# Sixteen gate weight tiles multiplied as eight pairs by seven block products

## The chip, the cores and the metric

The kernel runs on one core of a Trainium2 chip. Its time is the device time of one execution in microseconds (us); a kernel's time is the median of its runs. The engines named below are TensorE (PE, with its weight load PEld), VectorE (DVE), ScalarE (ACT), GpSimd (POOL) and SyncE (SP, which here only issues DMAs). Each engine works through its own instructions in order and waits for the others through semaphores.

## The reference, cut to what matters

One layer of a hybrid block: two token mixers over 512 latent tokens (after 256 context tokens), a gated merge of both, a residual with modulation, and a feed-forward stage. Width is 1024, all in fp32. The change touches the products of `u` (the normalised and modulated input) with the gate weights and what hangs on them:

```python
def merge(pp, o, h):                      # pp: the columns of u @ w_in
    y_gla = _head_rms_norm(o, gla_norm_g, u.dtype) * jax.nn.silu(pp[3])
    y_m = h * jax.nn.sigmoid(pp[8])
    gate_gla, gate_m = jnp.split(jax.nn.sigmoid(pp[10]), 2, axis=-1)
    y = gate_gla * (y_gla @ w_br_gla) + gate_m * (y_m @ w_br_mlstm)
    return y @ w_out
x = x + g1 * mix
x = x + g2 * _swiglu(_modulate(_rms_norm(x, norm2_g[i]), sh2, sc2), w_ffn_in[i], w_ffn_out[i])
```

`h` is the mLSTM scan's result; this scan runs over the tokens in column-major order. The vectors `g1`, `sh2`, `sc2`, `g2` are rows of `silu(c) @ w_ada + b_ada` (adaLN).

## The kernel before

**Products.** Features lie on the 128 partitions and tokens along the free axis. A fp32 factor is split into a high part (fp32r) and a low remainder, and a product is three matmuls, hi·hi, hi·lo and lo·hi (`mm3`, L243 to L245). A weight tile of 1024x128 is loaded by SP into a raw buffer (`wload`, L220, three buffers), ACT casts it to `whi` (L215), DVE subtracts to get `wlo` (L216); there are four buffers of each. A gate (`gate`, L880) is one weight tile against all 512 tokens: 8 times 3 matmuls of 512 columns into `ps_g`, then a sigmoid on ACT (L885 to L887). `u` stands in `ub`, from L929 on as `ucm`: 8 tiles in column-major token order, in each 512 columns of high and 512 of low part.

**Order of the stages.** At the start (to about 56 us) an order written by hand, the table `ORDER`, runs the modulation rows (`M..`, and the transposes `R0` to `R3` of their results into columns, L359), the normalisation and the steps that make `u` (`ut`, `uh`, `ul` and so on). Then come the projections and both scans. `head_norm` normalises the scan's output `mo`: an inverse root by Newton steps on 128x8 values (L178 to L180) and eight scalings (L666), each of 128x256. `to_feat` (L893) transposes the scan's output back to features and multiplies it with its gate and norm weight (`yf`, L902), and splits it: `yg` for the first branch, `ym` for the second.

Then `branch_a` (L983) runs eight times: a wp10 gate, a `wbg` product of `yg`, and their product `ya` (L989). `interleave` puts the 32 adaLN rows between its steps, four rows each (`ada_rows`, L968): SP loads 512 KB into `wr`, POOL multiplies with `crow` (L972), ACT sums up along the row into a column of `ada` (L973). Behind it stand eight wp8 gates (`p8`), `to_feat(mo, ...)` for `ym`, and eight times a wp10 gate, a `wbm` product of `ym`, their product and the sum with `ya` (branch B, `yb`). The output product `ps_wo`, the residual and the feed-forward stage follow. That stage multiplies pairs of 128-column weight tiles already by seven block products instead of eight (`Pair`, `prod`, `pair_slot`), with the order of PE, DVE and ACT written by hand (`tc.manual_schedule`).

**Who sets the order.** Outside such stretches a scheduler decides, with a model of the engines' times, where each instruction stands on its engine; it is fixed when the kernel is built. Buffers come from pools by tag: `blk` has 29 buffers for all its uses, `mid` 8, `tmp` 7; PSUM has four banks for `psm` and four for `psx`. A new tile waits until the last reader of the buffer's old tile is done.

Of the kernel before, what the change touches and what calls it, by code (L numbers as in the profile page):

```python
# [69 lines left out]
def block_kernel(ctx: ExitStack, tc: tile.TileContext, a, out):  # L70
# [818 lines left out]
    def halves(n, nm):  # L889
        bl_ = [blk(f"{nm}{i}") for i in range((n + 1) // 2)]  # L890
        return [bl_[i // 2][:, (i % 2) * 512:(i % 2) * 512 + 512] for i in range(n)]

    def to_feat(o_pairs, gate_, v0, nm):  # L893

        ys = []
        for j in range(8):
            ps = psx("ps_t" + nm)
            for t in range(4):
                o = (t % 2) * 512 + (j % 4) * P
                pe.transpose(ps[:, t * P:(t + 1) * P], o_pairs[j // 4][t // 2][:, o:o + P], ident)  # L900
            y = tmp("yf")[:, :512]
            vec.scalar_tensor_tensor(y, ps, vc(v0 + j), gate_[j], op0=ALU.mult, op1=ALU.mult)  # L902
# [95 lines left out]
    p8 = halves(8, "p8_")  # L998
# [124 lines left out]
    def prod(ps, w, x, first):

        for k in range(4):
            c, t = slice(k * P, k * P + P), slice(k * 256, k * 256 + 256)
            for i, (y, z) in enumerate(((0, 0), (0, 1), (1, 0))):
                pe.matmul(ps[:, :256], lhsT=w[y][:, c], rhs=x[z][:, t], start=first and k + i == 0,  # L1134
                          stop=k == 3 and i == 2, skip_group_check=not first)

    def flat(t):
        return t.rearrange("p k c -> p (k c)")

    class Pair:  # L1140


        def __init__(self, j):
            self.j = j
            self.raw = [flat(wload(a["wfi"][2 * j + i])[0]) for i in range(2)]
            self.b11, self.b21 = self.raw[0][:, :512], self.raw[0][:, 512:]
            self.b12, self.b22 = self.raw[1][:, :512], self.raw[1][:, 512:]
            self.g = {}

        def sums(self):  # L1150
            self.t21, self.t34 = blk("t21")[:, :1024], blk("t34")[:, :1024]
            self.t2, self.t1 = self.t21[:, :512], self.t21[:, 512:]
            self.t3, self.t4 = self.t34[:, :512], self.t34[:, 512:]

        def t(self, n):
            o, p_, q_ = {1: (self.t1, self.b11, self.b12), 2: (self.t2, self.t1, self.b22),
                         3: (self.t3, self.b12, self.b22), 4: (self.t4, self.t2, self.b21)}[n]
            vec.tensor_tensor(o, p_, q_, op=ALU.add)  # L1158

        def hi(self, n, early=False):  # L1160

            if n == 4:
                g4 = blk("g4", F32R)
                h, l, src = (g4[:, :512],), (g4[:, 512:1024],), (self.b22,)
            elif early:
                src = {1: lambda: (self.b11, self.b21), 2: lambda: (self.t2, self.t1)}[n]()
                h, l = ([bp.tile([P, EW], F32R, name=f"e{n}", tag="mid", bufs=8)[:, :512] for _ in range(2)]
                        for _ in range(2))
            else:
                src = ({1: lambda: self.raw[0], 2: lambda: self.t21, 3: lambda: self.t34}[n](),)  # L1170
                h = (flat(wp.tile([P, NK, P], F32R, name=f"g{n}h", tag="whi", bufs=NHI)),)
                l = (flat(wp.tile([P, NK, P], F32R, name=f"g{n}l", tag="wlo", bufs=NLO)),)
            self.g[n] = (h, l, src)
            for x, y in zip(h, src):
                act.copy(x, y)

        def lo(self, n):
            for h, l, src in zip(*self.g[n]):
                vec.tensor_tensor(l, src, h.bitcast(F32), op=ALU.subtract)

        def half(self, n, i=0):

            if len(self.g[n][0]) > 1 or n == 4:
                return self.g[n][0][i], self.g[n][1][i]
            return self.g[n][0][0][:, 512 * i:512 * i + 512], self.g[n][1][0][:, 512 * i:512 * i + 512]
# [298 lines left out]
```

## Time and profile before

| | before |
|---|---|
| median of 3 runs | 1093.02 us (1092.85 to 1093.86) |
| the profiled execution | 1093.14 us |
| its span in the trace | 1091.4 us |
| PE busy | 1070.8 us (98%), 5882 matmuls |
| DVE busy | 676.6 us (62%) |
| ACT busy | 536.8 us (49%) |
| POOL busy | 114.0 us (10%), of it the 32 adaLN rows 89.8 us |
| chain that ended last | PE 88%, DVE 4%, DMA 3%, ACT 2% |

The profile is one execution seen instruction by instruction. A row of its timeline reads: start and duration in us, engine, line, operation, output<-inputs by the program's names, shapes, count, and in brackets how long the engine had been idle before it and what ended that. `q` behind an engine's name is its queue of DMA issues. In this notation branch A runs until 549 us, the wp8 gates to 594, branch B from there to 686, the output product and the rest to the end.

### The profile page before, as it was taken

To read this page: it belongs to the slowest core of one execution; us is meant where nothing else is said; L and a number is where in the kernel's file an instruction comes from. 1 tells how busy PE (TensorE), PEld (TensorE's weight loads), DVE (VectorE), ACT (ScalarE), POOL (GpSimd) and SP (SyncE) were. 2 spreads that over 40 slices of the span, in tenths; PEclk is the share of its full clock that TensorE was granted. 3 is DMA by queue.
4 is the path that set the end of the run, shared out by engine and by line. 5 is a ranking of instruction groups with operands and counts; after the bars stand their busy time and mean duration, and the time that the engine had idled before them with its cause. 6 is when DMAs were issued, how large, how long until landed. Compare 5 with 4: busy or idle time off the path is not lost.

```text
span 1091.4 us, 14985 instructions
## 1 busy us (share of the span) xinstructions
PE 1070.8 (98%) x5882; PEld 909.3 (83%) x5882; DVE 676.6 (62%) x1192; ACT 536.8 (49%) x902; POOL 114.0 (10%) x57
## 2 busy tenths in 40 slices
PE   9899999999999999999999999999899999999996
PEld 3578888788888888888888888899899999988886
DVE  4867785964384484694234544569888888873333
ACT  5577655543272365366563323356565555742211
POOL 0000100200010000049980000000000000110000
PEclk9899999999999999999999999999999999999999
DMA  9612111021121121257764223601332333333212
GB/s 362 230 58 69 47 44 43 12 105 39 42 76 38 37 93 65 72 184 287 250 211 134 77 96 97 243 28 36 120 106 90 115 117 110 99 110 103 87 53 77
DMA packets 34270, 116.39 MB, mean 107 GB/s; under 512 B 3960, under 2 KB 6264, under 8 KB 34200
## 3 DMA queue, kind: packets, MB, share of 16 engines
q1 hardware_dynamic: 32672, 114.25, 31.1%
q10 hardware_dynamic: 1528, 1.19, 0.3%
q8 instruction: 46, 0.75, 0.3%
q14 instruction: 24, 0.20, 0.1%
HBM read 113.33 MB, written 2.10 MB: 106 GB/s over the span
## 4 chain that ended last, share of the span: by engine, by line
PE 88%; DVE 4%; DMA 3%; ACT 2%; issue 1%; SPq 0%; DVEq 0%; ACTq 0%
PE ps_X L1134 10%; PE ps_g L245 5%; PE ps_g L244 5%; PE ps_g L243 5%; PE ps_Z L1134 5%; PE ps_fo L245 4%; PE ps_fo L243 4%; PE ps_fo L244 4%; PE ps_v L428 3%; PE ps_v L430 3%; PE ps_v L429 3%; PE ps_br L245 3%; PE ps_br L244 3%; PE ps_br L243 3%; PE ps_Y L1134 2%; PE ps_mU L836 2%
## 5 line engine op out<-in xcount | busy, mean ns | idle before, releaser
L216 DVE TENSOR_TENSOR wlo<-wraw,whi 128x1024 fp32r<-128x1024 f32 (+1 forms) x110 | 140.8, 1283 | 142.6 <-ACT whi L215 141.2
L215 ACT CAST whi<-wraw 128x1024 fp32r<-128x1024 f32 (+1 forms) x110 | 113.2, 1035 | 184.3 <-PE ps_fo L244 71.1
L244 PE MATMUL ps_g<-ucm,whi 128*128 128x512 f32 x256 | 102.6, 401 | 0.0
L245 PE MATMUL ps_g<-ucm,wlo 128*128 128x512 f32 x256 | 102.0, 398 | 0.0
L243 PE MATMUL ps_g<-ucm,whi 128*128 128x512 f32 x256 | 101.5, 397 | 0.0
L972 POOL TENSOR_TENSOR wr<-wr,crow 128x1024 f32<-128x1024 f32 x32 | 89.8, 2842 | 65.8 <-ACT crow L965 65.8
L243 PE MATMUL ps_fo<-h,whi 128*128 128x512 f32 (+1 forms) x198 | 73.4, 371 | 0.0
L244 PE MATMUL ps_fo<-h,whi 128*128 128x512 f32 (+1 forms) x198 | 72.9, 369 | 0.0
L245 PE MATMUL ps_fo<-h,wlo 128*128 128x512 f32 (+1 forms) x198 | 72.9, 369 | 0.0
L244 PEld LDWEIGHTS ps_g<-ucm,whi 128*128 128x128 f32 x256 | 48.1, 188 | 11.2
L243 PEld LDWEIGHTS ps_g<-ucm,whi 128*128 128x128 f32 x256 | 48.1, 188 | 10.9
L245 PEld LDWEIGHTS ps_g<-ucm,wlo 128*128 128x128 f32 x256 | 48.1, 188 | 10.5
L973 ACT ACTIVATE wr<-wr 128x1024 f32<-128x1024 f32 x32 | 33.9, 1060 | 35.6 <-POOL wr L972 35.6
L1330 POOL TENSOR_TENSOR h<-hf,h 128x512 fp32r<-128x512 f32 x5 | 7.8, 1559 | 389.7 <-ACT h L1329 389.7
L244 PEld LDWEIGHTS ps_fo<-h,whi 128*128 128x128 f32 x198 | 37.2, 188 | 6.9
L245 PEld LDWEIGHTS ps_fo<-h,wlo 128*128 128x128 f32 x198 | 37.2, 188 | 6.8
L243 PEld LDWEIGHTS ps_fo<-h,whi 128*128 128x128 f32 x198 | 37.2, 188 | 6.8
L682 POOL TENSOR_SCALAR_AFFINE_SELECT a<-a 128x512 f32<-128x512 f32 x8 | 10.9, 1365 | 202.7 <-ACT a L679 202.6
L1134 PE MATMUL ps_Z<-s5h,g 128*128 128x256 f32 x160 | 31.6, 280 | 0.0
L1246 DVE TENSOR_TENSOR hf<-sl,cc 128x512 f32<-128x512 f32 x20 | 14.9, 747 | 23.4 <-ACT sl L1245 23.3
L1245 ACT ACTIVATE sl<-ps_X 128x256 f32<-128x256 f32 x20 | 7.7, 385 | 41.7 <-PE ps_X L1134 41.7
L1158 DVE TENSOR_TENSOR t<-t,wraw 128x512 f32<-128x512 f32 x40 | 27.6, 689 | 0.7
(475 smaller groups left out, 3157.1 us busy)
## 6 DMA issues: line engine op xcount, KB each, us to landing
wraw<-in_wfi SPq DMA_DIRECT2D x44, 512.0 KB, 3.6
wraw<-in_wp SPq DMA_DIRECT2D x32, 512.0 KB, 3.5
wr<-in_wada_b SPq DMA_DIRECT2D x32, 512.0 KB, 4.7
wa<-in_wada_a SPq DMA_DIRECT2D x16, 512.0 KB, 9.2
wraw<-in_wfo SPq DMA_DIRECT2D x16, 512.0 KB, 3.5
wraw<-in_wgv SPq DMA_DIRECT2D x8, 512.0 KB, 3.6
wraw<-in_wmqk SPq DMA_DIRECT2D x8, 512.0 KB, 3.5
wraw<-in_wmv SPq DMA_DIRECT2D x8, 512.0 KB, 4.1
```

Of the source, the lines that this page charges most:

```text
L215: act.copy(hi, src)
L216: vec.tensor_tensor(lo, src, hi.bitcast(F32), op=ALU.subtract)
L243: pe.matmul(ps, lhsT=wh, rhs=xh, start=first, stop=False)
L244: pe.matmul(ps, lhsT=wh, rhs=xl, start=False, stop=False)
L245: pe.matmul(ps, lhsT=wl, rhs=xh, start=False, stop=last)
L428: pe.matmul(ps, lhsT=h_, rhs=wh, start=(k == 0), stop=False)
L429: pe.matmul(ps, lhsT=h_, rhs=wl, start=False, stop=False)
L430: pe.matmul(ps, lhsT=l_, rhs=wh, start=False, stop=(k == NK - 1))
L972: pool.tensor_tensor(wr, wr, crow, op=ALU.mult)
L973: act.activation(wr, wr, AF.Identity, accum_out=ada[:, j:j + 1])
L1134: pe.matmul(ps[:, :256], lhsT=w[y][:, c], rhs=x[z][:, t], start=first and k + i == 0, stop=k == 3 and i == 2, skip_group_check=not first)
L1158: vec.tensor_tensor(o, p_, q_, op=ALU.add)
```

## The change

Four parts. First, the eight wp8 gates and the second eight wp10 gates are taken as eight pairs, in `gate_slot`, each with seven products of a 512x128 weight block and 256 tokens (12 matmuls of 256 columns each). Such a product needs sums of weight blocks (`Pair`, whose class moves up unchanged but for its source) and four sums and differences of token blocks, `su[1]`, `su[2]`, `su[3]`, `su[5]`. Second, a generator `s_gen` makes the token sums; it is chained behind `ada_rows` as the filler of branch A, and the rate goes from 4 to 6.5. `su[3]` is written over a part of `ucm` that is read no more (`s3_split`). Third, all gates come first: the transposes and products for `ym` are run within slots 5 and 6 and behind slot 7 (`feat_gen`), and then the eight `wbm` products, without gates between them. Fourth, in `ORDER`, `R0` and `T0` move up and three warm-up steps (matmuls on constants, nothing reads their result) are put in.

```diff
-    SQ5 ... M03 R2 ut7 ut6 uh7 T2
-    ut2 R0 uh6 ul7 T0 uh2 ul6 g7 S0 ...
+    SQ5 ... M03 R2 R0 ut7 ut6 uh7 T2
+    warm T0 warm warm ut2 uh6 ul7 uh2 ul6 g7 S0 ...
...
+    def s_gen():
...
+        f, f3 = blk("sf")[:, :1024], blk("sf3")[:, :1024]
+        gs[3] = f3
+        def diff(o, x, y):
+            d = tmp("sd")[:, :512].rearrange("p (h t) -> p h t", h=2)
+            vec.tensor_tensor(d, x, y, op=ALU.subtract)
+            vec.tensor_tensor(o, d[:, 0], d[:, 1], op=ALU.add)
+        def halve(n):
+            su[n] = [(units.pop(0), units.pop(0)) for _ in range(4)]
+            for k in range(4):
+                act.copy(su[n][k][0], f[:, 256 * k:256 * k + 256])
+                vec.tensor_tensor(su[n][k][1], f[...], su[n][k][0].bitcast(F32), op=ALU.subtract)
+        for k in range(4):
+            diff(f[:, 256 * k:256 * k + 256], part(k, B), part(k + 4, B))
+            yield
+        halve(1)
+        yield
+        for k in range(4):
+            diff(f3[:, 256 * k:256 * k + 256], part(k, A), part(k, B))
+            yield
+        for n, o, op in ((2, 0, ALU.subtract), (5, 4, ALU.add)):
+            for k in range(4):
+                for h in range(2):
+                    c = f[:, 256 * k:256 * k + 256]
+                    vec.tensor_tensor(c, c, part(k + o, A)[:, h], op=op)
+                yield
+            halve(n)
+            yield
+    def s3_split():
+        su[3] = [(ub[k][:, 256:512], ub[k][:, 768:1024]) for k in range(4)]
+        for k in range(4):
+            c = gs[3][:, 256 * k:256 * k + 256]
+            act.copy(su[3][k][0], c)
+            vec.tensor_tensor(su[3][k][1], c, su[3][k][0].bitcast(F32), op=ALU.subtract)
+    def gate_slot(w, nx, late, o0, o1):
...
+        prod(X, w.half(1), U11, True)
+        late()
+        act.copy(p1, X[:, :256])
...
+        prod(Y, w.half(1, 1), U12, True)
+        vec.tensor_tensor(p1, Y[:, :256], p1, op=ALU.add)
...
+        prod(X, w.half(2), su[2], False)
+        act.copy(u2, X[:, :256])
+        act.activation(o0[:, A], p1, AF.Sigmoid)
...
+        prod(Z, w.half(2, 1), su[1], True)
+        act.copy(q5, Z[:, :256])
...
+        prod(X, w.half(3), su[3], False)
+        act.copy(u3, X[:, :256])
...
+        vec.tensor_tensor(cc[:, B], q5, u3, op=ALU.subtract)
+        prod(Z, w.half(4), su[5], False)
+        vec.tensor_tensor(cc[:, A], Z[:, :256], u2, op=ALU.subtract)
+        prod(X, w.half(3, 1), U22, False)
+        def end():
+            act.activation(o0[:, B], X[:, :256], AF.Sigmoid)
+            act.activation(o1, cc[:, :512], AF.Sigmoid)
+        return end
-    interleave(branch_a(), ada_rows(), 4)
+    interleave(branch_a(), chain(ada_rows(), s_gen()), 6.5)
...
-    for j in range(8):
-        gate(a["wp8"][j], AF.Sigmoid, p8[j], False)
-    ym = to_feat(mo, p8, V_MN, "m")
+    feat = feat_gen(mo, p8, V_MN, "m", ym)
+    s3_split()
+    w = Pair(a["wp8"], 0)
...
+    with tc.manual_schedule(engines=MAN):
+        for j in range(8):
...
+            if j < 7:
+                nx = Pair(a["wp8"], j + 1) if j < 3 else Pair(a["wp10"], j + 1)
+            late = gate_slot(w, nx, late, *o)
+            if 4 < j < 7:
+                next(feat)
+                next(feat)
+            w = nx
+        late()
+    drain(feat)
...
-        pb = tmp("p10b")[:, :512]
-        gate(a["wp10"][8 + j], AF.Sigmoid, pb, False)
+        pb = pbs[j]
```

In `gate_slot`, `nx` is the next pair, whose sums (`t`), casts (`hi`) and subtractions (`lo`) stand between the products. The token sums are `sd` (a difference of 128x512, L1081 of the changed kernel), `sf` (the sum of its halves, L1082, and the running sums, L1102) and the parts of `su` (the cast L1087, the subtraction L1088).

**The first place: DVE at the start of branch A.** Before, DVE's order there is the end of the inverse root of `mo`'s norm (`rs_..`), the eight scalings of `mo`, and the first product `ya`; `wlo` ahead of the scalings is that of wbg[2], the last row is that of wp10[3].

```order
L180 SCALAR_TENSOR_TENSOR rs_yh<-rs_th,rs_yh 128x8
L216 TENSOR_TENSOR wlo<-wraw,whi 128x1024
L178 TENSOR_TENSOR rs_th<-rs_yh 128x8
L179 SCALAR_TENSOR_TENSOR rs_th<-rs_th,hv 128x8
L180 SCALAR_TENSOR_TENSOR rs_yh<-rs_th,rs_yh 128x8
L666 TENSOR_SCALAR mo_3087<-mo_3087,rs_yh 128x256 x4
L666 TENSOR_SCALAR mo_3088<-mo_3088,rs_yh 128x256 x4
L989 TENSOR_TENSOR ya_3771<-ps_br,ya_3771 128x512
L216 TENSOR_TENSOR wlo<-wraw,whi 128x1024
```

Of the change, the same place on DVE:

```order
L1081 TENSOR_TENSOR sd<-ucm_1730 128x512
L180 SCALAR_TENSOR_TENSOR rs_yh<-rs_th,rs_yh 128x8
L178 TENSOR_TENSOR rs_th<-rs_yh 128x8
L179 SCALAR_TENSOR_TENSOR rs_th<-rs_th,hv 128x8
L180 SCALAR_TENSOR_TENSOR rs_yh<-rs_th,rs_yh 128x8
L178 TENSOR_TENSOR rs_th<-rs_yh 128x8
L179 SCALAR_TENSOR_TENSOR rs_th<-rs_th,hv 128x8
L180 SCALAR_TENSOR_TENSOR rs_yh<-rs_th,rs_yh 128x8
L666 TENSOR_SCALAR mo_3093<-mo_3093,rs_yh 128x256 x4
L666 TENSOR_SCALAR mo_3094<-mo_3094,rs_yh 128x256 x4
L993 TENSOR_TENSOR ya_3777<-ps_br,ya_3777 128x512
L216 TENSOR_TENSOR wlo<-wraw,whi 128x1024
```

Seven of the eight differences `sd` now stand at or above the first row shown, among the last two subtractions of `yg` and the `wlo` of wbg[2], so that most of the root and all scalings come behind them. The seven hold all `tmp` buffers. On SP the load of wbg[4], which waits for the raw buffer that the `wlo` of wp10[3] (the last row) frees, stood behind row 8 of the adaLN rows and ahead of row 9; now it stands behind row 9 and ahead of row 10.

**The second place: the entry to slot 0, on DVE and ACT.** Before, DVE's stretch from the last product `ya` to the first `yf` of `ym` (`ps_tm`), past the sums of the adaLN columns (`ada`, `a2c`).

```order
L989 TENSOR_TENSOR ya_3774<-ps_br,ya_3774 128x512
L216 TENSOR_TENSOR wlo<-wraw,whi 128x1024 x2
L993 TENSOR_TENSOR ada<-ada,vcol 128x32
L996 SCALAR_TENSOR_TENSOR a2c<-ada,vcol 128x8
L216 TENSOR_TENSOR wlo<-wraw,whi 128x1024 x6
L902 SCALAR_TENSOR_TENSOR yf<-ps_tm,vcol,p_0_4418 128x512 x2
```

Of the change, DVE at the same place; `g1l` is the low part of the first pair, `t_4510` one of its weight sums, `sf_4302` is sf3:

```order
L993 TENSOR_TENSOR ya_3779<-ps_br,ya_3779 128x512 x2
L1054 TENSOR_TENSOR g1l<-wraw,g1h 128x1024
L1082 TENSOR_TENSOR sf<-sd 128x256 x4
L1081 TENSOR_TENSOR sd<-ucm_1733 128x512
L1088 TENSOR_TENSOR su<-sf,su 128x256 x3
L1102 TENSOR_TENSOR sf<-sf,ucm_1724 128x256
L1082 TENSOR_TENSOR sf_4302<-sd 128x256 x4
L1102 TENSOR_TENSOR sf<-sf,ucm_1727 128x256
L1088 TENSOR_TENSOR su<-sf,su 128x256
L1102 TENSOR_TENSOR sf<-sf,ucm_1730 128x256
L1033 TENSOR_TENSOR t_4510<-wraw 128x512
```

And ACT of the change there, with the additions of the last two adaLN rows (31 and 32, L977 now) and slot 0's copy of its first product (`e_4541<-ps_X`):

```order
L1112 CAST ucm_1730<-sf_4302 128x256
L1050 CAST g_4528<-wraw 128x512
L1112 CAST ucm_1733<-sf_4302 128x256
L977 ACTIVATE wr,ada<-wr 128x1024
L1087 CAST su<-sf 128x256
L977 ACTIVATE wr,ada<-wr 128x1024
L1087 CAST su<-sf 128x256
L1124 COPY e_4541<-ps_X 128x256
L1087 CAST su<-sf 128x256
L1050 CAST g2h<-t_4510 128x1024
```

The token sums stand ahead of the first pair's weight sums on DVE, and behind and between the last rows on ACT. `sf` takes the `blk` buffer of adaLN row 28, so it waits for that row's addition on ACT; sf3 takes that of row 29.

**The third place: TensorE at the start.** The transposes of the modulation rows (`pt`), then the first products of `u` (`ps_lr`); `wu` are the warm-up matmuls. Before:

```order
L359 MATMUL pt<-comb,r_357 128x2 x4
L359 MATMUL pt<-comb,r_371 128x2 x4
L243 MATMUL ps_lr<-u_153,whi 96x512
L244 MATMUL ps_lr<-u_153,whi 96x512
L245 MATMUL ps_lr<-u_153,wlo 96x512
```

Of the change:

```order
L359 MATMUL pt<-comb,r_357 128x2 x4
L299 MATMUL wu<-ones 128x128 x2
L359 MATMUL pt<-comb,r_359 128x2 x4
L299 MATMUL wu<-ones 128x128 x4
L243 MATMUL ps_lr<-u_153,whi 96x512
L244 MATMUL ps_lr<-u_153,whi 96x512
L245 MATMUL ps_lr<-u_153,wlo 96x512
```

Six warm-up matmuls now stand between the two groups of transposes and the first product.

More of the change, by code (lines that the diff above doesn't have):

```diff
@@ L990, in branch_a, with prod @@
             yield
-    interleave(branch_a(), ada_rows(), 4)
+    def prod(ps, w, x, first):
+        if len(x) == 2:
+            x = [[z[:, k * 256:k * 256 + 256] for z in x] for k in range(4)]
+        for k in range(4):
+            c = slice(k * P, k * P + P)
+            for i, (y, z) in enumerate(((0, 0), (0, 1), (1, 0))):
+                pe.matmul(ps[:, :256], lhsT=w[y][:, c], rhs=x[k][z], start=first and k + i == 0,
+                          stop=k == 3 and i == 2, skip_group_check=not first)
@@ new lines, in flat, with __init__, sums, t @@
+    def flat(t):
+        return t.rearrange("p k c -> p (k c)")
+    class Pair:
+        def __init__(self, src, j):
+            self.j = j
+            self.raw = [flat(wload(src[2 * j + i])[0]) for i in range(2)]
+            self.b11, self.b21 = self.raw[0][:, :512], self.raw[0][:, 512:]
+            self.b12, self.b22 = self.raw[1][:, :512], self.raw[1][:, 512:]
+            self.g = {}
+        def sums(self):
+            self.t21, self.t34 = blk("t21")[:, :1024], blk("t34")[:, :1024]
+            self.t2, self.t1 = self.t21[:, :512], self.t21[:, 512:]
+            self.t3, self.t4 = self.t34[:, :512], self.t34[:, 512:]
+        def t(self, n):
+            o, p_, q_ = {1: (self.t1, self.b11, self.b12), 2: (self.t2, self.t1, self.b22),
+                         3: (self.t3, self.b12, self.b22), 4: (self.t4, self.t2, self.b21)}[n]
+            vec.tensor_tensor(o, p_, q_, op=ALU.add)
+        def hi(self, n, early=False):
+            if n == 4:
+                g4 = blk("g4", F32R)
+                h, l, src = (g4[:, :512],), (g4[:, 512:1024],), (self.b22,)
+            elif early:
+                src = {1: lambda: (self.b11, self.b21), 2: lambda: (self.t2, self.t1)}[n]()
+                h, l = ([bp.tile([P, EW], F32R, name=f"e{n}", tag="mid", bufs=8)[:, :512] for _ in range(2)]
+                        for _ in range(2))
+            else:
+                src = ({1: lambda: self.raw[0], 2: lambda: self.t21, 3: lambda: self.t34}[n](),)
+                h = (flat(wp.tile([P, NK, P], F32R, name=f"g{n}h", tag="whi", bufs=NHI)),)
+                l = (flat(wp.tile([P, NK, P], F32R, name=f"g{n}l", tag="wlo", bufs=NLO)),)
+            self.g[n] = (h, l, src)
+            for x, y in zip(h, src):
+                act.copy(x, y)
+        def lo(self, n):
+            for h, l, src in zip(*self.g[n]):
+                vec.tensor_tensor(l, src, h.bitcast(F32), op=ALU.subtract)
+        def half(self, n, i=0):
+            if len(self.g[n][0]) > 1 or n == 4:
+                return self.g[n][0][i], self.g[n][1][i]
+            return self.g[n][0][0][:, 512 * i:512 * i + 512], self.g[n][1][0][:, 512 * i:512 * i + 512]
@@ new lines, in block_kernel, with part @@
+    MAN = {mybir.EngineType.PE, mybir.EngineType.DVE, mybir.EngineType.Activation}
+    A, B = slice(0, 256), slice(256, 512)
+    gs = {}
+    su = {}
+    def s_gen():
+        def part(k, s):
+            return ub[k][:, :1024].bitcast(F32).rearrange("p (h t) -> p h t", h=2)[:, :, s]
+        units = []
+        for i in range(8):
+            t = bp.tile([P, EW], F32R, name="su", tag="mid", bufs=8)
+            units += [t[:, 256 * n:256 * n + 256] for n in range(3)]
+        f, f3 = blk("sf")[:, :1024], blk("sf3")[:, :1024]
[8 more added lines that the diff above has]
+                act.copy(su[n][k][0], f[:, 256 * k:256 * k + 256])
+                vec.tensor_tensor(su[n][k][1], f[:, 256 * k:256 * k + 256], su[n][k][0].bitcast(F32), op=ALU.subtract)
+        for k in range(4):
[13 more added lines that the diff above has]
+            halve(n)
+            yield
@@ L996, in block_kernel @@
     vec.scalar_tensor_tensor(a2c, sc2c, 1.0, vc(V_N2, 8), op0=ALU.add, op1=ALU.mult)
[L998 to L1001 removed]
+    p8, pbs, ym = [], [], []
+    feat = feat_gen(mo, p8, V_MN, "m", ym)
+    s3_split()
+    w = Pair(a["wp8"], 0)
+    w.sums()
+    for n in (1, 3, 2, 4):
+        w.t(n)
+    for n in (1, 2, 3, 4):
+        w.hi(n)
+        w.lo(n)
+    with tc.manual_schedule(engines=MAN):
+        late = lambda: None
+        for j in range(8):
+            t = blk(f"gt{j}")
+            o = [t[:, 0:512], t[:, 512:1024]]
+            (p8 if j < 4 else pbs).extend(o)
+            nx = None
+            if j < 7:
[7 more added lines that the diff above has]
+    drain(feat)
     yb = []
     for j in range(8):
[L1004 to L1005 removed]
+        pb = pbs[j]
         w = wtile(a["wbm"][j])
@@ L1127, in s_lo @@
         vec.tensor_tensor(sb[n][2], sb[n][0], sb[n][1].bitcast(F32), op=ALU.subtract)
[L1129 to L1185, printed above, removed]
```

38 lines of the change are left out of this document (31 added, 7 removed).

## The prediction

> **What bounds the kernel now.** I read the page's busy table, then the busy time by stretches from the branch stage on, then single instructions where the change begins.
>
> ```profile
> PE 1070.8 (98%) x5882; PEld 909.3 (83%) x5882; DVE 676.6 (62%) x1192; ACT 536.8 (49%) x902; POOL 114.0 (10%) x57
> ```
> ```profile
> 480.00:500.00 20.00, 20.00 (x88) 16.18 (x87) 18.97 (x10) 12.64 (x19) 20.00 (x8) 1.00 0.48 174
> ...
> 540.00:560.00 20.00, 20.00 (x88) 16.20 (x87) 5.08 (x5) 11.64 (x19) 20.00 (x8) 1.00 0.88 303
> 560.00:580.00 20.00, 20.00 (x88) 16.21 (x87) 7.84 (x8) 12.82 (x19) 8.33 (x4) 1.00 0.45 141
> ```
>
> The columns are the stretch, its length, the busy time of PE, PEld, DVE, ACT and POOL, then clock and DMA. TensorE is the bound, without a gap and at full clock, through branch A, the gates and branch B. In the same stretches POOL is full as well: it multiplies the 32 adaLN rows, until 568.3 (its group is below). Nothing on TensorE needs those rows until the next residual, so that costs nothing today. DVE has room after 500, hardly any before.
>
> **The products.** TensorE's timeline at the first wp8 gate, at the first transpose behind the eight, and at the first output product; then the chain of waits in the feed-forward stage, which does the same seven products already.
>
> ```profile
> 549.22 0.39 PE L243 MATMUL ps_g<-ucm,whi 128*128 128x512 f32 x1
> ...
> 593.66 0.38 PE L900 MATMUL ps_tm<-ident,mo 128*128 128x128 f32 x2
> ...
> 686.12 0.40 PE L243 MATMUL ps_wo<-yb,whi 128*128 128x512 f32 x1
> ```
> ```profile
> 788.25 2.83 PE ps_X L1134 x24
> ...
> 798.14 2.85 PE ps_X L1134 x24
> ```
>
> Eight gate tiles take 593.66 - 549.22 = 44.4 us, sixteen 88.9. A pair slot takes 798.14 - 788.25 = 9.89 us, eight 79.1. The change removes **9.8 us** of TensorE time if every slot runs as those do. Casts, subtractions and half sums of a slot are theirs too, without the last multiplication; the normalisations and splits of ym add some 2.6 us of DVE to the slots 6 and 7 each. I cost them at nothing, since DVE has about 2 us to spare in a slot, and at up to 3 us in the range.
>
> With E for the end of gate slot 0, the output products start at E plus seven slots (69.2), eight branch B tiles (44.4) and the transposes (686.12 - 593.66 - 88.9 = 3.6), together E + 117.2. Undelayed, E would be 549.22 + 9.89 = 559.1. The question is E.
>
> **POOL and DVE exclude each other.** POOL's one group; DVE's timeline at the head norm's scalings around POOL's start; a weight subtraction beside POOL and one without it; the tile view of a small operation of the inverse root (minimum/median/maximum in ns).
>
> ```profile
> 478.57 89.76 POOL L972 TENSOR_TENSOR wr<-wr,crow 128x1024 f32<-128x1024 f32 x32 [65.81 <-ACT crow L965]
> ```
> ```profile
> 477.38 0.35 DVE L666 TENSOR_SCALAR mo<-mo,rs_yh 128x256 f32<-128x256 f32 x1
> ...
> 478.70 2.51 DVE L666 TENSOR_SCALAR mo<-mo,rs_yh 128x256 f32<-128x256 f32 x1
> ...
> 481.14 2.50 DVE L666 TENSOR_SCALAR mo<-mo,rs_yh 128x256 f32<-128x256 f32 x1
> ...
> 486.57 2.83 DVE L216 TENSOR_TENSOR wlo<-wraw,whi 128x1024 fp32r<-128x1024 f32 x1
> ...
> 589.16 1.23 DVE L216 TENSOR_TENSOR wlo<-wraw,whi 128x1024 fp32r<-128x1024 f32 x1 [4.33 <-ACT whi L215]
> ```
> ```profile
> L178 DVE TENSOR_TENSOR rs_th<-rs_yh x12: 157/166/436, 176.7 to 476.8; 128x8 f32<-128x8 f32 x12
> ```
>
> A scaling takes 0.35 us, 0.27 from one to the next, until POOL begins; then 2.5, and it ends when a row ends. While POOL has rows, DVE gets one such operation per row, 2.43 us apart. Today five of the eight scalings are done before POOL starts.
>
> The small operations of the root stood beside POOL only once (the 436). I take all of them to wait; their lower bound, that only L178 waits, brings the next step 1.2 us earlier. The Trainium skill (SBUF — State Buffer, Who interferes with whom) says that a DVE instruction with two SBUF inputs and a GpSimd instruction that reads SBUF block each other for the whole instruction; by it L179 and L180 wait as well. The scalings agree (2.51 against 0.35).
>
> **Stall one, in branch A.** DVE, TensorE and SyncE before, where the seven early differences go in:
>
> ```profile
> 470.65 1.41 DVE L902 SCALAR_TENSOR_TENSOR yf<-ps_tg,vcol,p 128x512 f32<-128x512 f32 x2
> ```
> ```profile
> 494.02 0.40 PE L245 MATMUL ps_g<-ucm,wlo 128*128 128x512 f32 x1
> ```
> ```profile
> 489.43 0.33 SPq L220 DMA_DIRECT2D wraw<-in_wbg  x1
> ```
> ```profile
> wr<-in_wada_b SPq DMA_DIRECT2D x32, 512.0 KB, 4.7
> ```
>
> From 472.0 DVE now has seven differences and two yg subtractions of 0.61, a weight subtraction of 1.15 and two small ones before the rest of the root: 472.0 + 5.5 + 1.15 + 0.3 = 478.9, just when POOL starts. So seven small operations and all eight scalings wait behind a row each. That would be 15 rows, but only 9 are there: the load of row 10 stands on SP behind wbg[4], which waits for the raw buffer that the subtraction of wp10[3] frees (today's 489.43 comes straight after 486.57 + 2.83). So POOL runs dry at 478.9 + 9 x 2.43 = 500.8; six scalings (1.6), a product of branch A (0.6) and the subtraction (1.15) end at **504.2**. Gate 3 wants that at 494.02, so TensorE stands 10 us and branch A ends near 560. That by itself is no term, as the next wait ends later; but row 10 lands only at 504.2 + 0.4 + 4.7 = 509.3.
>
> **Stall two, in slot 0.** ACT adds the rows up; here rows 1, 28 and 32 (the first column is the start):
>
> ```profile
> 481.10 1.06 ACT L973 ACTIVATE wr<-wr 128x1024 f32<-128x1024 f32 x1 [1.16 <-POOL wr L972]
> ...
> 557.93 1.06 ACT L973 ACTIVATE wr<-wr 128x1024 f32<-128x1024 f32 x1 [2.10 <-POOL wr L972]
> ...
> 568.49 1.05 ACT L973 ACTIVATE wr<-wr 128x1024 f32<-128x1024 f32 x1
> ```
>
> The pace is (557.93 - 481.10) / 27 = 2.85 us a row, with the weight subtractions among them, as will be so again. Row 28 is multiplied at 509.3 + 19 x 2.85 = 563.4 and added up, with the accumulator's read of 0.19, at 564.7. Only then does the first sf on DVE go (second place above: it waits for that row's buffer), and with it, in DVE's order, everything that slot 0 needs from its third product on. Rows 29 to 32 let through one addition each, at 2.5: POOL is done at 573.4, DVE free at 573.8. ACT's copy of the first product, which the third overwrites, stands behind row 32 too, but ACT keeps up from there. DVE's prices in the same work, from the chain of waits in the feed-forward stage:
>
> ```profile
> 759.58 1.14 DVE g3l L1179
> 760.71 0.60 DVE g L1179
> ...
> 770.50 0.34 DVE cc L1239
> ```
>
> From there to the last low half of su[5], which the sixth product needs, DVE has 4 operations of 1024 columns (4.6), 12 of 512 (7.3), 37 of 256 (12.6) and two tiny ones (0.3): 24.8 us, to 598.6. The last three matmuls of that product and the seventh add 1.8: 600.4. Long idle brings the half clock (next part), for which I take 1.5 of at most 3.4 us. **E = 602**, so stall two is 602 - 559.1 = **+42.9 us**. Ends: if stall one costs POOL nothing, row 28 stays at 557.93 + 1.25, POOL ends at 569, E = 596 (+37); if rows come every 2.43, the fastest that is shown, POOL ends at 557 and E is 584 (+25); with 3.4 for the clock and 3 for the slots, 607 (+48).
>
> **The start.** TensorE's clock and pitch around the transposes of the modulation rows:
>
> ```profile
> 43.00:50.00 7.00, 6.42 (x19) 5.18 (x20) 6.96 (x14) 3.55 (x7) 0.00 (x0) 0.51 0.54 181
> ```
> ```profile
> 43.59 1.86 PE L359 MATMUL pt<-comb,r 4*128 4x2 f32 x8 [2.34 <-ACT r L354]
> ...
> 45.91 0.63 PE L244 MATMUL ps_lr<-u,whi 128*96 128x512 f32 x1
> 46.34 0.63 PE L245 MATMUL ps_lr<-u,wlo 128*96 128x512 f32 x1
> ...
> 50.58 0.39 PE L244 MATMUL ps_lr<-u,whi 128*96 128x512 f32 x1
> 50.81 0.40 PE L245 MATMUL ps_lr<-u,wlo 128*96 128x512 f32 x1
> ```
>
> R0 moved up and the filler matmuls close the 2.34 us gap; ten matmuls at 0.43 instead of 0.24 cost 2 us. DVE does a weight subtraction earlier, which delays u by 0.7 and is given back by the third tile. I take **-2.0**, between -2.4 and +0.5. The Trainium skill (TensorE: Matmul & The Clock Gate, Part 1) has the clock fall after an idle window of about 3.4 us; by that the gap of 2.34 should not have cost it, and the fillers would give about -0.3. Here it did fall, with tiny transposes around the gap.
>
> **Sum.** -9.8 - 2.0 + 42.9 = +31.1 us on the profiled execution's 1093.14 (span 1091.4 and 1.7 around it), which is 0.1 above the median shown: **1124 us**.
>
> **Rivals.**
> - *Faster, about 1081* (-9.8 - 2.0). One mechanism: POOL's rows are over before slot 0 asks. For a draw, DVE must be free of POOL by 543, which takes some 2.0 us a row without a pause; below that the gain appears. For it: the page calls POOL's spans rough. Against it: ACT's additions, on another engine, give the same 2.85, and the shortest spacing is 2.43. Chance 0.08.
> - *POOL without loss, about 1106* (-11.8 + 25): the differences and small operations slip past POOL, no row is missing, E = 584. Against it: each DVE row beside POOL above. Chance 0.10.
> - *The slots don't run as in the feed-forward stage, over 1136*: DVE falls behind in each of them by 0.7 us or more, atop stall two. Against it: DVE's spare 2 us. Chance 0.05.
> - *The stall is there, but just pays for the gain*: 0.02.
>
> **How the numbers follow.** My forecast has 0.75, and around it the bounds 1117 to 1131. For 8 in 10 the range takes in the second rival and a little above: 1106 to 1136. A measurement can tell about 0.2% from no change. Slower by more: 0.75 + 0.10 + 0.05 = 0.90; within: 0.02; faster: 0.08.
>
> **What would show it.** In the new profile: POOL's rows in two groups, with a gap near 500 to 509; the eight scalings of L666 at about 2.5 us; TensorE idle some 10 us before gate 3's first wlo, and 20 us or more within ps_X of slot 0, put down to DVE or ACT; the first sf right behind the 28th row's addition; seven later slots of 9.9 us each; no 0.5 clock at 43 to 50. I am wrong if sf and su are done before branch A ends, or POOL's last row is over by 545. If only stall one is missing, the time is near 1118.

## The result and the profile after

| | before | after |
|---|---|---|
| median | 1093.28 us (1092.85 to 1093.86, 4 runs) | 1124.28 us (1122.30 to 1126.06, 4 runs) |
| the profiled execution / its span | 1093.14 / 1091.4 us | 1122.49 / 1120.8 us |
| ratio to before | | 1.0282, 95% interval 1.0269 to 1.0295 |

The change makes the kernel 2.8% slower, by 31.0 us. The four times after lie in two groups, 1122.3 to 1122.5 and twice 1126.1; the profile is of the lower group.

The page's busy table after, and the busy time by stretches (stretch, length, PE, PEld, DVE, ACT, POOL, clock, DMA share, GB/s):

```profile
PE 1074.5 (96%) x6182; PEld 925.5 (83%) x6182; DVE 756.1 (67%) x1312; ACT 567.0 (51%) x974; POOL 108.0 (10%) x57
```
```profile
480.00:500.00 20.00, 11.36 (x50) 8.92 (x48) 19.79 (x16) 8.37 (x13) 17.40 (x8) 0.89 0.17 52
500.00:520.00 20.00, 20.00 (x75) 15.71 (x76) 11.53 (x9) 13.33 (x21) 14.22 (x5) 0.86 0.91 345
520.00:540.00 20.00, 16.27 (x71) 12.81 (x69) 6.29 (x4) 11.46 (x19) 20.00 (x9) 1.00 0.93 316
540.00:560.00 20.00, 18.22 (x69) 14.62 (x70) 5.72 (x5) 11.20 (x19) 20.00 (x8) 0.83 0.68 205
560.00:580.00 20.00, 12.17 (x55) 9.93 (x53) 20.00 (x34) 11.22 (x25) 8.30 (x4) 0.85 0.04 10
580.00:600.00 20.00, 15.30 (x95) 14.63 (x95) 18.93 (x36) 10.73 (x19) 0.00 (x0) 0.72 0.32 99
600.00:620.00 20.00, 20.00 (x172) 20.00 (x171) 15.57 (x23) 12.35 (x22) 0.00 (x0) 1.00 0.35 106
```

TensorE, without a gap there before, is short in every stretch from 480 to 600 except one, and gets less than the full clock in five of six; from 600 on it is full again. So the loss lies in branch A and slot 0.

**Stall one.** POOL and DVE where the differences went in, and TensorE's waits in branch A (timelines; in brackets the idle time and what ended it):

```profile
476.14 21.26 POOL L976 TENSOR_TENSOR wr<-wr,crow 128x1024 f32<-128x1024 f32 x9 [65.80 <-ACT crow L969]
505.78 5.65 POOL L976 TENSOR_TENSOR wr<-wr,crow 128x1024 f32<-128x1024 f32 x2 [8.38 <-DMA wr<-in_wada_b]
```
```profile
475.05 1.28 DVE L1081 TENSOR_TENSOR sd<-ucm 128x512 f32<-128x512 f32 x2
476.25 2.39 DVE L180 SCALAR_TENSOR_TENSOR rs_yh<-rs_th,rs_yh 128x8 f32<-128x8 f32 x1
478.67 2.32 DVE L178 TENSOR_TENSOR rs_th<-rs_yh 128x8 f32<-128x8 f32 x1
481.03 2.33 DVE L179 SCALAR_TENSOR_TENSOR rs_th<-rs_th,hv 128x8 f32<-128x8 f32 x1
...
490.49 2.29 DVE L180 SCALAR_TENSOR_TENSOR rs_yh<-rs_th,rs_yh 128x8 f32<-128x8 f32 x1
492.82 6.31 DVE L666 TENSOR_SCALAR mo<-mo,rs_yh 128x256 f32<-128x256 f32 x8
```
```profile
499.87 0.77 PE L243 MATMUL ps_g<-ucm,whi 128*128 128x512 f32 x1 [8.64 <-DVE ya L993]
...
541.78 0.79 PE L243 MATMUL ps_g<-ucm,whi 128*128 128x512 f32 x1 [5.52 <-ACT ya L885]
```

Nine rows, then POOL is dry for 8.4 us, since row 10 isn't loaded. Seven operations on 128x8 values take 2.3 to 2.4 us each, one to a row, and two scalings too; the other six go through at 0.34 when POOL is dry. The Trainium skill (SBUF — State Buffer, Who interferes with whom) names DVE instructions with two SBUF inputs for this; the rows of L178 to L180 agree with it. The scalings wait as well, though they read one tensor and a column of factors, so they do not bear it out by themselves. Not every operation is held: the products `ya`, which read one factor from PSUM, take 0.68 us beside POOL's rows. In the kernel before:

```profile
485.97 0.68 DVE L989 TENSOR_TENSOR ya<-ps_br,ya 128x512 f32<-128x512 f32 x1
```

TensorE waits 8.6 us. A second wait of 5.5 us, at 541.78, is for a sigmoid on ACT; the prediction did not have it.

**Stall two.** POOL's last rows, ACT's addition of row 28, DVE from the first sf to the last low half of su, and TensorE in slot 0:

```profile
552.59 15.71 POOL L976 TENSOR_TENSOR wr<-wr,crow 128x1024 f32<-128x1024 f32 x6
```
```profile
558.39 1.06 ACT L977 ACTIVATE wr<-wr 128x1024 f32<-128x1024 f32 x1 [1.22 <-POOL wr L976]
559.35 0.19 ACT L977 ACTIVATION_READ_ACCUMULATOR wr<-wr 128x1 f32 x1
```
```profile
559.57 9.01 DVE L1082 TENSOR_TENSOR sf<-sd 128x256 f32<-128x256 f32 x4 [5.85 <-ACT wr L977]
568.51 0.68 DVE L1081 TENSOR_TENSOR sd<-ucm 128x512 f32<-128x512 f32 x1
...
570.45 1.42 DVE L1082 TENSOR_TENSOR sf<-sd 128x256 f32<-128x256 f32 x4
...
592.52 0.42 DVE L1088 TENSOR_TENSOR su<-sf,su 128x256 fp32r<-128x256 f32 x1
```
```profile
569.57 0.51 PE L1009 MATMUL ps_X<-ucm,g1h 128*128 128x256 f32 x2 [3.05 <-ACT ya L885]
578.76 0.58 PE L1009 MATMUL ps_X<-su,g2h 128*128 128x256 f32 x1 [4.57 <-ACT g2h L1050]
...
582.40 0.58 PE L1009 MATMUL ps_X<-su,g2l 128*128 128x256 f32 x1 [2.27 <-DVE g2l L1054]
...
595.80 0.40 PE L1009 MATMUL ps_X<-ucm,g1h 128*128 128x256 f32 x2
```

The first sf starts 0.03 us behind the read of row 28's accumulator. Four of them take 9.0 us beside the last rows; the other four, behind POOL's end, take 1.4. From 568.5 (POOL's end is 568.3) DVE works without a pause to 592.9, while TensorE waits for one weight part after another, often at half clock (0.58 for a matmul that takes 0.28). Slot 1 begins at 595.80.

### The profile page after: what moved, and what is told of

It reads as the page before. It is cut to its first block, busy times and chain, and to the rows that moved or that the text cites. A ratio compares the mean times of both kernels' runs of the same rounds, so it can differ in the third digit from the quotient of the medians.

```text
span 1120.8 us, 15763 instructions
## 1 busy us (share of the span) xinstructions
PE 1074.5 (96%) x6182; PEld 925.5 (83%) x6182; DVE 756.1 (67%) x1312; ACT 567.0 (51%) x974; POOL 108.0 (10%) x57
## 4 chain that ended last, share of the span: by engine, by line
PE 76%; DVE 11%; DMA 4%; ACT 4%; POOL 2%; issue 2%; SPq 0%; DVEq 0%; ACTq 0%; POOLq 0%
PE ps_X L1009 13%; PE ps_Z L1009 7%; PE ps_fo L243 4%; PE ps_fo L245 4%; PE ps_fo L244 4%; PE ps_v L428 3%; PE ps_Y L1009 3%; PE ps_v L430 3%; PE ps_v L429 3%; PE ps_g L243 2%; PE ps_g L245 2%; PE ps_g L244 2%; POOL wr L976 2%; PE ps_mU L836 2%; PE ps_br L243 2%
## 5 line engine op out<-in xcount | busy, mean ns | idle before, releaser
L216 DVE TENSOR_TENSOR wlo<-wraw,whi 128x1024 fp32r<-128x1024 f32 (+1 forms) x94 | 119.1, 1269 | 84.2 <-ACT whi L215 82.8
L215 ACT CAST whi<-wraw 128x1024 fp32r<-128x1024 f32 (+1 forms) x94 | 96.4, 1033 | 154.8 <-PE ps_fo L244 70.9
L976 POOL TENSOR_TENSOR wr<-wr,crow 128x1024 f32<-128x1024 f32 x32 | 83.8, 2657 | 74.2 <-ACT crow L969 65.8
L243 PE MATMUL ps_g<-ucm,whi 128*128 128x512 f32 x128 | 53.6, 419 | 14.2 <-DVE ya L993 8.6
L244 PE MATMUL ps_g<-ucm,whi 128*128 128x512 f32 x128 | 53.9, 421 | 0.0
L245 PE MATMUL ps_g<-ucm,wlo 128*128 128x512 f32 x128 | 53.2, 416 | 0.0
L977 ACT ACTIVATE wr<-wr 128x1024 f32<-128x1024 f32 x32 | 33.9, 1059 | 22.4 <-POOL wr L976 22.3
L243 PEld LDWEIGHTS ps_g<-ucm,whi 128*128 128x128 f32 x128 | 25.3, 197 | 20.5 <-issue 9.0
L1054 DVE TENSOR_TENSOR g1l<-wraw,g1h 128x1024 fp32r<-128x1024 f32 x27 | 34.6, 1281 | 7.7 <-ACT g1h L1050 7.7
L1054 DVE TENSOR_TENSOR g3l<-t,g3h 128x1024 fp32r<-128x1024 f32 x28 | 34.2, 1223 | 7.6 <-ACT g3h L1050 7.6
L1033 DVE TENSOR_TENSOR t<-wraw 128x512 f32<-128x512 f32 x56 | 36.1, 683 | 0.0
L1050 ACT CAST g2h<-t 128x1024 fp32r<-128x1024 f32 x27 | 28.4, 1051 | 8.9 <-DVE t L1033 8.8
L1054 DVE TENSOR_TENSOR g2l<-t,g2h 128x1024 fp32r<-128x1024 f32 x27 | 32.9, 1217 | 0.0
```

What stands on the lines that cost most here:

```text
L215: act.copy(hi, src)
L216: vec.tensor_tensor(lo, src, hi.bitcast(F32), op=ALU.subtract)
L243: pe.matmul(ps, lhsT=wh, rhs=xh, start=first, stop=False)
L244: pe.matmul(ps, lhsT=wh, rhs=xl, start=False, stop=False)
L245: pe.matmul(ps, lhsT=wl, rhs=xh, start=False, stop=last)
L976: pool.tensor_tensor(wr, wr, crow, op=ALU.mult)
```

## Experiments

Kernels that were run together shared the runs of the kernel before (medians 1093.3 to 1093.6 us). A table of the decisive ones stands at the end of this section.

**POOL's multiplication taken out.** Without it the modulation rows are wrong.

```diff
             sync.dma_start(wr, a["wada_b"][:, j, :])
-            pool.tensor_tensor(wr, wr, crow, op=ALU.mult)
             act.activation(wr, wr, AF.Identity, accum_out=ada[:, j:j + 1])
```

> The change without POOL's multiplication of the 32 adaLN rows (ACT adds up the rows as they were loaded, so the modulation rows are wrong). Theory: the whole loss comes from DVE and POOL excluding each other. Without POOL the head norm's scalings take 0.35 us each, TensorE does not stand before gate 3, and the token sums are done when slot 0 asks: 1093.3 - 9.8 - 2.0 = 1081 us, between 1079 and 1085. Rival: the 24.8 us of token sums on DVE behind branch A are too much by themselves, or the pair slots do not reach 9.9 us: above 1090.

Measured: 1084.27 us (1084.15 to 1086.28), ratio 0.9921 (0.9906 to 0.9935). DVE's order there is still root and scalings behind seven differences:

```profile
477.54 2.19 DVE L666 TENSOR_SCALAR mo<-mo,rs_yh 128x256 f32<-128x256 f32 x8
```

Eight scalings in 2.2 us instead of 6.3, and no wait of TensorE in branch A. The 40 us between this kernel and the change come with POOL's multiplication. The run does not split these 40 us: without it DVE is not held, and the rows also reach ACT sooner and give their buffers back sooner.

**The token sums taken out, with and without POOL.** `su` is taken from the column-major tiles as they are, so the gates are wrong; the rows run at rate 4.

```diff
-    interleave(branch_a(), chain(ada_rows(), s_gen()), 6.5)
+    interleave(branch_a(), ada_rows(), 4)
+    for n in (1, 2, 3, 5):
+        su[n] = [(ub[k][:, 256:512], ub[k][:, 768:1024]) for k in range(4)]
-    s3_split()
```

> The change without the token sums: su is taken from the column-major tiles as they are, s_gen and s3_split are left out, the rows stay on POOL at rate 4 (the gates are wrong). Theory (POOL holds every DVE operation, not the token sums alone): branch A ends near 547, POOL at 566, and the first pair's own four sums and its low parts still go one to a row, so slot 0 ends 5 to 14 us late: 1086 to 1096. Rival (the token sums are the whole price, other DVE work gets through): 1080 to 1084.

Measured: 1105.50 us (1104.01 to 1105.83), outside both. The direction is the theory's, the size was too small: ACT's copy of slot 0's first product stands behind rows' additions, and the first pair's own sums go one to a row, so that the third product starts only behind POOL's last row (565.9):

```profile
566.13 0.80 PE L1009 MATMUL ps_X<-ucm,g2h 128*128 128x256 f32 x2 [14.87 <-ACT e L1124]
```

The first of those sums had itself waited 9.9 us, until 553.8, for an earlier row's addition on ACT.

> The change without the token sums (su taken from the column-major tiles as they are) and without POOL's multiplication: the fourth corner beside the change (1124.3), no_mult (1084.3) and no_sums (1105.5). Theory: without POOL the token sums on DVE are hidden behind branch A, so leaving them out as well changes little: 1081 to 1085. Rival (the token sums cost time by themselves, and their price adds to POOL's): the same 18.8 us as with POOL come off, 1065 to 1070.

Measured: 1084.58 us (1084.35 to 1085.66). So the token sums cost 18.8 us beside POOL's rows (1124.28 - 1105.50) and nothing without them (1084.27 against 1084.58). Of the 40 us, 21 are there even without token sums: in this kernel a pair slot that begins while POOL has rows pays by itself.

**The rows on DVE instead of POOL**, and the same in the kernel before.

```diff
-            pool.tensor_tensor(wr, wr, crow, op=ALU.mult)
+            vec.tensor_tensor(wr, wr, crow, op=ALU.mult)
```

> The change with the 32 row multiplications on DVE instead of POOL, nothing left out. Theory (POOL and DVE exclude each other): DVE gets 32 x 1.13 = 36 us more work and the kernel still becomes much faster, since an operation of DVE no longer waits for a row of 2.4 us; DVE's work from 469.6 is some 66 us, then 24.8 of token sums, so slot 0 ends near 563 and the time is 1087, between 1081 and 1095. Rival (DVE simply has too much to do before slot 0): 36 us more on DVE make it slower, 1130 to 1160.

Measured: 1094.78 us (1093.04 to 1095.86, 10 runs), ratio 1.0009 (1.0000 to 1.0019): 29.5 us off the change, though DVE has 39 us more to do (32 rows of 1.22). The rival falls. But the time is at the upper edge of what was expected: slot 0 still waits for DVE and for a copy on ACT.

```profile
554.37 0.58 PE L1009 MATMUL ps_X<-su,g2h 128*128 128x256 f32 x1 [2.17 <-DVE su L1088]
561.06 0.79 PE L1009 MATMUL ps_X<-ucm,g3h 128*128 128x256 f32 x2 [2.30 <-ACT e L1138]
```

> The kernel before, with all 32 row multiplications on DVE instead of POOL. Theory: in the kernel before, the rows on POOL cost nothing, as nothing in branch A and the gates wants more of DVE than it gets between the rows; so there is nothing to win there, 1092 to 1095. Rival (POOL's rows already cost the kernel before something, and the faster version below the change owes its gain to that): below 1091.

Measured: 1094.08 us (1093.67 to 1095.00, 10 runs), ratio 1.0006 (0.9997 to 1.0016). In the kernel before, the rows on POOL cost nothing, as the prediction says.

**Only 24 rows in branch A**, the eight of g2 ahead of the output of the feed-forward stage (which loads and activates `crow` again), once on POOL and once on DVE.

```diff
-    def ada_rows():
-        for j in range(32):
+    def ada_rows(j0=0, j1=24):
+        for j in range(j0, j1):
...
+    crow = blk("crow")[:, :D]
+    sync.dma_start(crow, a["crow"].partition_broadcast(P))
+    act.activation(crow, crow, AF.Silu)
+    drain(ada_rows(24, 32))
+    vec.tensor_tensor(g2c, g2c, vc(V_BADA + 40, 8), op=ALU.add)
     acc3 = blk("acc3")[:, :512]
```

> The change with only 24 adaLN rows in branch A, still on POOL; the last eight (g2, needed only at the output of the feed-forward stage) are multiplied on POOL just ahead of that output. Nothing is left out. Theory (slot 0 ends some 27 us after POOL's last row, whatever else happens before): eight rows of 2.6 us fewer bring POOL's end, and with it slot 0's, 21 us earlier, 1124.3 - 21 = 1103, between 1099 and 1108. Rival (the loss is DVE's work of 24.8 us behind branch A, or the buffers): POOL's end does not matter and the time stays above 1115.

Measured: 1110.32 us (1108.78 to 1112.43), 14 less than the change instead of 21, outside both the theory and the rival. POOL's last row of branch A ended at 549.2, 19 us earlier, and slot 0 waited for nothing any more; but it began only at 573.6, since TensorE had stood twice before:

```profile
501.30 0.77 PE L243 MATMUL ps_g<-ucm,whi 128*128 128x512 f32 x1 [8.67 <-DVE ya L993]
548.94 0.80 PE L243 MATMUL ps_g<-ucm,whi 128*128 128x512 f32 x1 [11.63 <-ACT ya L885]
```

Once stall two is shorter, stall one and the wait for the sigmoid set the end. The waits in branch A and stall two are no sum but a maximum, as the prediction has it for stall one.

> As the kernel with all rows on DVE, but only 24 of them in branch A, and the last eight (g2) on DVE ahead of the feed-forward stage's output, where DVE has room. Theory: what was left of the loss there (1094.8 against 1084.3 without any multiplication) is DVE's own work before slot 0, 8 x 1.13 = 9 us less of it give 1094.8 - 9 = 1086, between 1083 and 1089, faster than both kernels. Rival (what was left is ACT's additions or the loads, or the eight rows cost as much where they go): 1092 to 1096.

Measured: **1085.79 us** (1085.14 to 1088.38, 5 runs), ratio 0.9935 (0.9922 to 0.9948): faster than both kernels. Eight rows less on DVE took 9.0 us off, as worked out (8 x 1.13); as the five runs spread over 3.2 us, the agreement is closer than they can show. From branch A to the output products TensorE has one wait left, 1.3 us between two later slots; slot 0 follows the last product of branch A at once:

```profile
548.68 0.40 PE L245 MATMUL ps_br<-yg,wlo 128*128 128x512 f32 x1
548.91 0.40 PE L1009 MATMUL ps_X<-ucm,g1h 128*128 128x256 f32 x2
```

**Stall one alone taken away**: the eight differences get buffers that come free only behind rows 24 to 27.

```diff
-            d = tmp("sd")[:, :512].rearrange("p (h t) -> p h t", h=2)
+            d = dd.pop(0).rearrange("p (h t) -> p h t", h=2)
...
+        dd = [t[:, s:s + 512] for t in [blk(f"sd{i}") for i in range(4)] for s in (0, 512)]
         f, f3 = blk("sf")[:, :1024], blk("sf3")[:, :1024]
```

> The change with the eight differences sd in buffers that come free only behind rows 24 to 27, so that they cannot go ahead of the root and the scalings: stall one alone is taken away. Theory as seen in the trace of the change (POOL's last row ends at 568 with or without stall one): the eight scalings cost 0.35 us each, TensorE runs through branch A without the 8.6 us, which ends near 547, and slot 0 still ends within 3 us of 595.8: 1121 to 1126. By the prediction's numbers (stall one puts POOL back by 5 us): 1118. Rival (TensorE's waiting in branch A adds up with that in slot 0): 1105 to 1112.

Measured: 1125.15 us (1124.13 to 1127.00), ratio 1.0292 (1.0277 to 1.0307). The end doesn't move, as expected of the trace, against the prediction's 1118. The test is not clean, though: POOL's last row did end 3.0 us earlier than in the change (565.3), and the differences, moved behind it, take that back (below the table). And branch A did not end near 547:

```profile
526.03 0.40 PE L245 MATMUL ps_br<-yg,wlo 128*128 128x512 f32 x1
538.28 0.80 PE L243 MATMUL ps_g<-ucm,whi 128*128 128x512 f32 x1 [11.86 <-ACT ya L885]
```

With POOL's rows never dry, the wait for the sigmoid is 11.9 us.

**Rate 4 instead of 6.5**, to take that wait away.

```diff
-    interleave(branch_a(), chain(ada_rows(), s_gen()), 6.5)
+    interleave(branch_a(), chain(ada_rows(), s_gen()), 4)
```

> The change with the filler's rate back from 6.5 to 4: ACT's order then has each gate's sigmoid behind at most three rows' additions, where the change has the two of the third ya pair behind eleven. Theory (slot 0 waits for POOL's last row and what DVE has left then; TensorE's 5.5 us of waiting for a sigmoid in branch A lies ahead of that wait and costs nothing in this kernel): those 5.5 us go, slot 0 ends within 3 us of where it does, 1121 to 1126. Rival (the waits in branch A add to the end): 1116 to 1119.

Measured: 1127.85 us (1126.51 to 1129.78), ratio 1.0315 (1.0301 to 1.0329). The wait for the sigmoid is gone (at most five additions stand between two sigmoids on ACT, thirteen in the change), which shows that it comes from ACT's order; the end is not earlier but 3.6 us later, beyond the theory's bounds and on the side away from the rival. POOL was dry for 11.7 us in this kernel, and its last row ended at 573.1, 4.8 later than in the change. The end follows that.

**sf in buffers of its own.**

```diff
-        f, f3 = blk("sf")[:, :1024], blk("sf3")[:, :1024]
...
+    f, f3 = blk("sf")[:, :1024], blk("sf3")[:, :1024]
     def ada_rows():
```

> The change with sf and sf3 allocated ahead of the adaLN rows, so that they do not wait for the buffers of rows 28 and 29; DVE's order is the same as in the change. Theory (it is POOL's running that holds DVE, the buffer only comes on top): sf starts some 6 us earlier, at 553 to 554, but two to three operations more pass until POOL ends, so 1 us is gained at most: 1121 to 1125. Rival (the wait for the row's buffer is the price, as the words of the prediction on stall two put it): the chain of 24.8 us starts 6 us earlier, and the time falls by as much, to 1116 to 1119.

Measured: 1122.42 us (1122.35 to 1124.51). This tells nothing: sf still takes its buffer where it is first written, and waits for the same row.

```profile
559.71 9.02 DVE L1083 TENSOR_TENSOR sf<-sd 128x256 f32<-128x256 f32 x4 [5.84 <-ACT wr L979]
```

What that buffer costs by itself stays open.

**The new start alone.** The kernel before with the changed `ORDER` and nothing else of the change.

> The kernel before with the new start alone (R0 and T0 moved up, three warm-up steps). By the prediction -2.0, between -2.4 and +0.5. The profiled executions show the first products of u at full clock in three of the kernels with the new start and at half clock in two, about 1.9 us apart; theory: its executions lie in two groups, 1090.9 and 1092.8, so the median is between 1090.5 and 1093. Rival (the new start always closes the gap): all between 1090.3 and 1091.5.

Measured: 1092.20 us over 11 runs, ratio 0.9984 (0.9975 to 0.9993), in two groups: five from 1090.61 to 1091.15 and six from 1092.20 to 1093.44.

**More filler at the start**, in the fastest version: three more warm-up steps behind T0 in `ORDER`.

> The version with 24 rows in branch A and 8 ahead of the output, all on DVE, with three more warm-up steps (six matmuls of 128 columns) behind T0. Theory: the two groups of its times (1085.1 to 1085.8 and 1087.8 to 1088.4) are the start at full and at half clock; more filler keeps the clock up and all executions lie between 1085 and 1086.5. Rival (the clock falls by something else than how long TensorE idles there, since it fell with 0.9 us of idle time in front): the two groups stay.

Measured: 1088.50 us (1087.47 to 1090.05). The theory falls. In its profile the clock at 43 to 50 us is 1.00 (0.53 in the profile of the version without the filler) and the output products start 2.3 us earlier (675.78 against 678.05), but the span is no shorter (1086.2 against 1086.0). Of that, 1.2 us are lost in the first slots of the feed-forward stage, where TensorE waits 3.1 us for a copy on ACT (1.9 without the filler). Why, where the rest goes, and what makes the upper group of the fastest version, is not settled.

| kernel | POOL's last row in branch A ends | first output product | median |
|---|---|---|---|
| the change | 568.3 | 714.8 | 1124.28 |
| differences late | 565.3 | 717.9 | 1125.15 |
| rate 4 | 573.1 | 719.8 | 1127.85 |
| 24 rows, POOL | 549.2 | 702.8 | 1110.32 |
| without token sums | 565.9 | 696.8 | 1105.50 |
| without POOL's multiplication | – | 676.7 | 1084.27 |
| without either | – | 676.0 | 1084.58 |
| rows on DVE | – | 686.5 | 1094.78 |
| 24 rows, DVE | – | 678.0 | 1085.79 |

From POOL's last row to the first output product the change and rate 4 take 146.5 and 146.7 us; with the differences late it is 152.6. There DVE's chain behind POOL's end takes 29.9 us instead of 24.4: five more differences (5 x 0.61 = 3.1 us) and two more sums (0.7) stand in it, and the rest is not traced.

## Why the prediction was right

The time forecast was 1124, the median is 1124.28. The mechanism held; that the number is met to 0.3 us is luck, as shown below. Point by point, in the profiled execution (29.4 us longer in its span):

- **Products.** -9.8 stands. With slot 0 no longer waiting (1084.3 without POOL's multiplication), 9.0 of the 11.8 us of products and start show; 2.1 of the rest are two waits for copies on ACT. Later slots were costed at nothing more; from slot 0's end to the output products it is 714.8 - 595.8 = 119.0, not 117.2. Of these 1.8 us, 1.3 are one wait, where the first products for ym go between the slots.
- **POOL and DVE exclude each other.** Right. That POOL's multiplication beside DVE is the cause is shown by 40 us without it, and by 29.5 with the rows on DVE, which then has more work. How much of this is the exclusion itself, and how much is that buffers and ACT's additions follow POOL's pace, no run splits: in the trace sf waits 5.9 us for row 28's addition, and then the exclusion costs its first four 7.6 us (9.0 against 1.4). All small operations of the root that met a row wait, as was taken.
- **Stall one.** Right in its kind and nearly in size: dry for 8.4 us (forecast 8.5), TensorE waits 8.6 (forecast 10), the weight subtraction ends at 500.9 (forecast 504.2). That it is no term by itself agrees with the kernel with the differences late, but that kernel does not show it cleanly: 3.0 us at POOL's end were won and lost again.
- **Stall two.** Right in its kind; this is the term that was mis-sized. Row 28 was added up at 559.5, not 564.7. The step that failed is "the pace is 2.85 us a row, as will be so again": the 32 rows take 83.8 us without the pause (2.62 each) instead of 89.8 (2.81), 6.0 us less; the likely reason is that DVE work done while POOL is dry lengthens no row. With a start 2.4 us earlier that makes just the 8.4 us that POOL was dry, and its last row ends at 568.3 as it did before, which is chance. So E is 595.8, the lower bound that was given for stall one costing POOL nothing (596). DVE's chain behind it took 24.4 us (568.5 to 592.9), forecast 24.8, and from there to slot 1 it was 2.9 us, forecast 3.3 (1.8, and 1.5 for the clock). The prediction's two lower ends, 596 and 584, leave out the 1.5 for the clock without saying so.
- **The start.** -2.4 at the first branch product (462.3 against 464.7) in this execution; alone it is worth 0.16% (1.7 us by the ratio, 1.4 by the medians), in two groups. Full clock at 43 to 50 us came true in this execution, but only in some of those profiled with the same start (0.53 to 0.77 in the others).
- **What made the sum fit.** 36.7 for slot 0 (start included, forecast 40.9), -9.8, +1.8 in the slots, +0.7 behind them: 29.4. The profiled execution belongs to the lower group of times; the upper one, 3.6 us later, brings the median up to the forecast, at a time that no execution had. What the upper group does differently no profile shows.
- **What was missed.** The wait for a sigmoid on ACT behind thirteen rows' additions. No run shows that it costs the change anything (from POOL's last row on, rate 4 takes the same time without it), but with POOL's end earlier it helps to set the time (24 rows on POOL). With it branch A ended later than the forecast's 560, so that slot 0 began at 569.6 and TensorE was idle within ps_X of slot 0 for 9.1 us, not for 20 or more.

The rival "POOL without loss" (1106) is ruled out by the rows beside POOL, "faster" by POOL's end at 568.3, "slots over 1136" by slots that begin 9.9 us apart behind slot 0.

## What to carry to other kernels

Before filling an engine's free time, ask what blocks it there: DVE looked free in the stretches at 500 to 580 (busy for 4.5 to 7.8 of every 20 us), but next to a running POOL it got one operation per row wherever the operation read only SBUF, however small. So 24.8 us of work, which are 55 operations, don't fit beside 32 rows. Count such room in operations, not in busy time. And when several waits lie on the way to one point, only the last counts until it is shortened; then the one before it sets the time, so a remedy is sized against both.

## What was not expected of the hardware

**The clock can fall with less than 1 us of idle time.** With the new start, six of eleven executions of the kernel with the start alone lie in the slower group. TensorE in two profiles with the same order, first the change, then the rows on DVE:

```profile
42.84 1.16 PE L299 MATMUL wu<-ones 128*128 128x128 f32 x8
44.02 0.48 PE L243 MATMUL ps_lr<-u,whi 128*96 128x512 f32 x1
45.25 0.47 PE L244 MATMUL ps_lr<-u,whi 128*96 128x512 f32 x1 [0.76 <-DVE u L379]
45.56 0.39 PE L245 MATMUL ps_lr<-u,wlo 128*96 128x512 f32 x1
```
```profile
43.04 1.16 PE L299 MATMUL wu<-ones 128*128 128x128 f32 x8
44.38 0.47 PE L243 MATMUL ps_lr<-u,whi 128*96 128x512 f32 x1 [0.18 <-ACT u L376]
45.62 0.74 PE L244 MATMUL ps_lr<-u,whi 128*96 128x512 f32 x1 [0.76 <-DVE u L379]
46.15 0.63 PE L245 MATMUL ps_lr<-u,wlo 128*96 128x512 f32 x1
```

The same idle time of 0.76 us stands ahead of the matmul that runs at full clock in one and at half clock in the other; nor do the 0.2 us just ahead of it set the two apart, as the kernel without POOL's multiplication has 0.18 and 0.77 us at these places and runs at full clock. What does is not in these rows. The Trainium skill (TensorE: Matmul & The Clock Gate, Part 1) has the clock fall after a free-running window of about 3.4 us of idle time; that the same kernel can go either way agrees with a window that runs free, but here TensorE was idle for at most 0.76 us in one piece between 40 and 46 us.

**A dry POOL made its rows shorter.** A DVE operation beside a row seems to lengthen it by about its own time (a row is 2.3 to 2.4 us alone and beside 128x8 operations, 3.4 with a weight subtraction inside), so a pause in which DVE catches up is partly given back.
